# A second, fp32r transpose of the attention latents, fed by word copies and checked into the residual

## The chip, the cores and the metric

The kernel runs on one core of one Trainium2 chip. The metric is the device time of one execution in microseconds (us). The kernel before was run three times: 2292.96, 2293.53 and 2295.82 us, so its time is the median, 2293.53 us. One more execution was profiled; everything that is said of single instructions comes from that one.

## The reference, cut to what matters

The reference is a trunk of two layers, an attention layer (MLA) and a Mamba-2 layer, each followed by a squared-ReLU MLP, on a residual stream x of 256 tokens by 2048 features, all in fp32. The change lies in the attention layer, where the input is projected to two latents of 512 features each, which are normalised and projected again:

```python
a = h @ w_in
c_q, c_kv, k_rope = jnp.split(a, [Q_LORA_RANK, Q_LORA_RANK + KV_LORA_RANK], axis=-1)
q = (rms_norm(c_q, q_norm_g) @ w_uq).reshape(B, S, MLA_HEADS, QK_HEAD_DIM)
kv = (rms_norm(c_kv, kv_norm_g) @ w_ukv).reshape(B, S, MLA_HEADS, QK_NOPE_DIM + V_HEAD_DIM)
...
x = x + mix
```

c_q and c_kv are the latents. mix is the output of the attention, and x the residual to which it is added.

## The kernel before, in words

All products of fp32 operands are made of fp32r matmuls: each operand is split into a rounded half (h, type fp32r) and the rest (lo = value - h), and three products h·h, lo·h and h·lo are summed. Weights arrive by DMA from the SP queue (L85) into six raw buffers, ScalarE rounds them (L102, wh), VectorE subtracts (L103, wl), and TensorE uses them (L325, L326, L329 in `block`). Loads run six units of weights ahead of TensorE and conversions three; there are four buffers each for wh and wl, so ScalarE and VectorE stop when TensorE hasn't freed one.

The order on TensorE is that of the program text. The other engines' order is set when the kernel is built, by a scheduler that follows the program's order but lets an instruction that it reckons to be ready go first. Each engine then runs its list in order.

The 256 tokens are two tiles of 128 (t = 0 and 1). A latent is 128 x 512 for each tile. Small pieces of work that need time before TensorE can go on are put off with `later(n, fn)`: fn is run after n more blocks, between two blocks. The stage around the change goes like this on TensorE:

- four blocks give the q latent (key "ain q"), then a narrow product ("ain r", L344), then four blocks give the kv latent ("ain c")
- `latent` (L781) takes the two accumulators: ScalarE sums squares (L296), VectorE and GpSimd make the reciprocal root (L282, L283, L789), VectorE scales the accumulator into a scratch tile cn (L794). It returns two functions, one for each token tile, that call `transposes`
- for the q latent, the two functions are put off with `later(3, fn)`, so they run after the third of the four "ain c" blocks, and after them the fold of the narrow product (L352) on the same tick; then comes the fourth "ain c" block
- for the kv latent, they run in the middle of the second q projection, `s0q(1)`, after the first of its two weight units; then follow the second unit and the first kv projection `s0kv(0)`, whose operands are the transposed latents (ckv)

`transposed` (L307) takes one PSUM bank, makes four 128 x 128 fp32 transposes into it (L310), and `split_out` lets ScalarE write the rounded half h from the bank (L299) and VectorE the rest lo (L300). A bank comes from `bank(wide)`: with wide true every second one is from the pool yp (two banks), otherwise it is from the pool sm (two banks). The q latent is transposed with wide true, the kv latent with wide false.

GpSimd (POOL) does the powers (L283, L290), the rotary tables and the rotary products (L764 to L779), and in this stage issues no DMA. Its first DMA in the kernel comes at 310 us (L199).

Of the kernel before, what the change touches and what calls it, by code (L numbers as in the profile page):

```python
# [20 lines left out]
F32 = mybir.dt.float32  # L21
F32R = mybir.dt.float32r
I32 = mybir.dt.int32
AF = mybir.ActivationFunctionType
ALU = mybir.AluOpType
# [3 lines left out]
P = 128  # L29
# [185 lines left out]
class Trunk:  # L215
# [565 lines left out]
    def latent(self, accs, gain, tiles, wide=True):  # L781

        nc = self.nc
        ssq = self.stat(2)
        for t in range(2):
            self.square_sum(accs[t], ssq[:, t:t + 1], scale=self.rs[t])
        r = self.rsqrt(ssq, 2, 512)
        r2 = self.stat(2)
        nc.vector.tensor_tensor(r2, r, self.rs_pool[(self.phase - 1) % 2][:, 0:2], ALU.mult)  # L789
        g = self.gain_tile(gain)  # L790
        fns = []
        for t in range(2):
            cn = self.scratch()
            nc.vector.scalar_tensor_tensor(cn, accs[t], r2[:, t:t + 1], g, ALU.mult, ALU.mult)  # L794
            fns.append(lambda t=t, cn=cn: self.transposes(cn, tiles[0], tiles[1], t, wide))
        return fns

    def mla(self, gain):
# [4 lines left out]

    def mla_body(self, mp, gain):
        nc, d = self.nc, self.d
        cq = [mp.tile([P, 4, 256], F32R, name=f"cq{i}") for i in range(2)]
        ckv = [mp.tile([P, 4, 256], F32R, name=f"ckv{i}") for i in range(2)]
        mk = mp.tile([P, 256], F32, name="mk")
# [29 lines left out]
        lat = self.latent(accs, d["kvg"], ckv, False)  # L838
# [725 lines left out]
```

## Time and profile before

| | us |
|---|---|
| median of three runs | 2293.53 |
| lowest and highest run | 2292.96, 2295.82 |
| the profiled execution, its own time | 2294.05 |
| its span from first to last instruction | 2292.3 |

The 1.75 us between the span and the execution's own time lie around the instructions. In rows of the profile, the line of the code stands first, then engine, operation, and the tiles as out<-in. A row of the timeline has the start, the duration, and the number of instructions that were merged. TensorE's matmuls overlap: a row shows 0.39 us for one of 512 columns, but the next starts 0.23 us later, so starts are compared, not durations. A transpose shows 0.27 us and is followed by the next after 0.11 us. "wh", "wl", "cq", "ckv", "s" (scratch, which cn is), "sm", "yp" and "acc" are the program's names of tiles.

### The profile page before, as it was taken

Reading aid. Unit: us, or ns where it says so; the run is one execution under the profiler, and the core shown is the slowest. Engines: PE = TensorE matmul, PEld = TensorE weight load, DVE = VectorE, ACT = ScalarE, POOL = GpSimd, SP = SyncE. Lnnn points to the kernel's source line nnn. Section 1 sums busy time; section 2 is a strip of 40 time slices with the busy share of each in tenths; the row PEclk is TensorE's granted clock in tenths of the full one; section 3 lists DMA queues with packets and bytes.
Section 4 is the critical chain, followed back from the end, with each engine's and each line's share of the span. In section 5 each row is a group of like instructions: output and inputs, shape, how many; then the busy total and the mean of one; then the engine's idle time right before and its main releaser. Section 6 shows DMA issues by size and latency. Waiting matters only on the chain.

```text
span 2292.3 us, 30455 instructions
## 1 busy us (share of the span) xinstructions
PE 2283.9 (100%) x10929; PEld 1898.4 (83%) x10929; DVE 1907.0 (83%) x2318; ACT 1392.6 (61%) x1947; POOL 212.7 (9%) x229
## 2 busy tenths in 40 slices
PE   9999999999999999999999999999999999999999
PEld 7898888888888888888888888888888888888887
DVE  7785698999899898687898688676989889989895
ACT  7775476566566666564666545544666666666663
POOL 1430000000000000000133112120000000000000
PEclk9999999999999999999999999999999999999999
DMA  8445687877887878667877777666687788888874
GB/s 315 151 126 155 198 230 249 261 242 252 262 242 247 262 215 275 201 209 241 283 262 264 253 265 256 228 197 200 208 258 233 244 267 244 249 267 239 249 226 163
DMA packets 161912, 538.07 MB, mean 235 GB/s; under 512 B 17680, under 2 KB 26832, under 8 KB 160736
## 3 DMA queue, kind: packets, MB, share of 16 engines
q1 hardware_dynamic: 151264, 502.44, 66.2%
q0 software_dynamic: 8096, 29.41, 7.9%
q10 hardware_dynamic: 2400, 4.27, 0.5%
q8 instruction: 86, 1.41, 0.3%
q14 instruction: 66, 0.54, 0.1%
HBM read 529.65 MB, written 6.41 MB: 234 GB/s over the span
## 4 chain that ended last, share of the span: by engine, by line
PE 97%; DMA 1%; DVE 1%; issue 0%; ACT 0%; SPq 0%; DVEq 0%
PE acc L325 13%; PE acc L326 13%; PE acc L329 13%; PE yp L595 9%; PE yp L596 9%; PE yp L594 9%; PE st L595 7%; PE st L596 7%; PE st L594 7%; PE sm L310 2%; DMA wraw<-mi 1%; DVE wl L103 1%; PE y L1280 1%; PE acc L594 1%; PE acc L596 1%; PE acc L595 1%
## 5 line engine op out<-in xcount | busy, mean ns | idle before, releaser
L102 ACT ACTIVATE wh<-wraw 128x1024 fp32r<-128x1024 f32 (+1 forms) x818 | 858.2, 1053 | 607.3 <-PE acc L326 284.3
L103 DVE TENSOR_TENSOR wl<-wraw,wh 128x1024 fp32r<-128x1024 f32 (+1 forms) x818 | 986.4, 1221 | 230.2 <-ACT wh L102 220.8
L595 PE MATMUL yp<-wl,k 128*128 128x512 f32 x896 | 348.9, 389 | 2.0 <-DVE wl L103 2.0
L594 PE MATMUL yp<-wh,k 128*128 128x512 f32 x896 | 349.8, 390 | 0.0
L596 PE MATMUL yp<-wh,k 128*128 128x512 f32 x896 | 348.8, 389 | 0.0
L325 PE MATMUL acc<-wh,xt 128*128 128x512 f32 x704 | 279.1, 397 | 0.9 <-ACT wh L102 0.9
L326 PE MATMUL acc<-wh,xt 128*128 128x512 f32 x704 | 274.5, 390 | 0.3 <-DVE xt L463 0.3
L102 ACT ACTIVATE wh<-wrx 128x1024 fp32r<-128x1024 f32 x168 | 177.9, 1059 | 136.0 <-PE yp L596 107.1
L103 DVE TENSOR_TENSOR wl<-wrx,wh 128x1024 fp32r<-128x1024 f32 x168 | 204.4, 1222 | 35.6 <-ACT wh L102 35.3
L595 PEld LDWEIGHTS yp<-wl,k 128*128 128x128 f32 x896 | 168.2, 188 | 37.4 <-DVE wl L103 2.8
L596 PEld LDWEIGHTS yp<-wh,k 128*128 128x128 f32 x896 | 168.2, 188 | 35.0
L594 PEld LDWEIGHTS yp<-wh,k 128*128 128x128 f32 x896 | 168.2, 188 | 34.7
L325 PE MATMUL acc<-wh,k 128*128 128x512 f32 x496 | 196.5, 396 | 0.0
L326 PE MATMUL acc<-wh,k 128*128 128x512 f32 x496 | 193.2, 390 | 0.0
L329 PE MATMUL acc<-wl,xt 128*128 128x512 f32 x704 | 188.3, 389 | 0.0
L594 PE MATMUL st<-wh,xt 128*128 128x512 f32 x448 | 176.8, 395 | 0.0
L595 PE MATMUL st<-wl,xt 128*128 128x512 f32 x448 | 174.8, 390 | 0.0
L596 PE MATMUL st<-wh,xt 128*128 128x512 f32 x448 | 174.8, 390 | 0.0
L325 PEld LDWEIGHTS acc<-wh,xt 128*128 128x128 f32 x704 | 132.3, 188 | 29.9 <-ACT wh L102 2.2
L326 PEld LDWEIGHTS acc<-wh,xt 128*128 128x128 f32 x704 | 132.3, 188 | 28.5 <-issue 1.2
L329 PEld LDWEIGHTS acc<-wl,xt 128*128 128x128 f32 x704 | 132.2, 188 | 27.7
L199 POOL DMA_DIRECT2D wrx<-mi x56 | 49.1, 876 | 1142.1 <-DVE wl L103 1036.1
(307 smaller groups left out, 3447.9 us busy)
## 6 DMA issues: line engine op xcount, KB each, us to landing
wraw<-mi SPq DMA_DIRECT2D x256, 512.0 KB, 5.3
wraw<-mo SPq DMA_DIRECT2D x256, 512.0 KB, 5.5
wraw<-si SPq DMA_DIRECT2D x160, 512.0 KB, 4.9
wraw<-so SPq DMA_DIRECT2D x64, 512.0 KB, 4.8
wrx<-mi SPq DMA_DIRECT2D x56, 512.0 KB, 5.3
wrx<-mi POOLq DMA_DIRECT2D x56, 512.0 KB, 8.2
wraw<-wo SPq DMA_DIRECT2D x32, 512.0 KB, 3.8
taps<-xD SPq DMA_DIRECT2D x16, 768.0 KB, 8.7
```

What stands on the lines that cost most here:

```text
L102: self.last = nc.scalar.activation(h[:, v], raw[:, v], AF.Copy)
L103: self.last_lo = nc.vector.tensor_tensor(lo[:, v], raw[:, v], h[:, v].bitcast(F32), ALU.subtract)
L199: nc.gpsimd.dma_start(st["b11"].tile, quarter(d, 1, 0), accum_op=ALU.add)
L310: self.nc.tensor.transpose(b[:, j * P:(j + 1) * P], src[:, j * P:(j + 1) * P], self.ident)
L325: nc.tensor.matmul(accs[t][:, :n], ah, wh[:, q, :], start=first and kt + q == 0, stop=False)
L326: nc.tensor.matmul(accs[t][:, :n], al, wh[:, q, :], start=False, stop=False)
L329: nc.tensor.matmul(accs[t][:, :n], lhs(kt + q, t)[0], wl[:, q, :], start=False, stop=en and q == nk - 1)
L594: nc.tensor.matmul(b, ah, wh, start=first and q == 0, stop=False)
L595: nc.tensor.matmul(b, ah, wl, start=False, stop=False)
L596: nc.tensor.matmul(b, al, wh, start=False, stop=last and q == 1)
L1280: nc.tensor.matmul(y[t][c, o], part(t)[:, c], xg[g][t][:, o], start=True, stop=True)
```

## The change: what it does

For each latent and token tile, a GpSimd DMA copies cn word for word into a new tile q of type fp32r. Where the tile was transposed once, it is now transposed twice: first q, as fp32r with an fp32r identity, into one bank, which ScalarE copies to a tile e; then cn, as fp32 as before, into another bank. VectorE subtracts the second bank from e, adds 2^60 times that difference to the first 512 columns of the residual tile, and then the second bank is split into h and lo as before. Both banks are of the pool sm, also for the q latent. The difference is zero if the fp32r transpose passes every word unchanged. The fp32r identity is made by a copy on GpSimd one block after the start.

```diff
         for t in range(2):
             cn = self.scratch()
             nc.vector.scalar_tensor_tensor(cn, accs[t], r2[:, t:t + 1], g, ALU.mult, ALU.mult)
-            fns.append(lambda t=t, cn=cn: self.transposes(cn, tiles[0], tiles[1], t, wide))
+            q = self.lat_pool.tile([P, 512], F32R, tag="lat", name=self.name("lat"), bufs=4)
+            nc.gpsimd.dma_start(q.bitcast(F32), cn)
+
+            def both(t=t, cn=cn, q=q):
+                b = self.bank(False)
+                for j in range(4):
+                    nc.tensor.transpose(b.bitcast(F32R)[:, j * P:(j + 1) * P], q[:, j * P:(j + 1) * P], self.ident_r)
+                e = self.lat_pool.tile([P, 512], F32, tag="late", name=self.name("late"), bufs=2)
+                nc.scalar.activation(e, b, AF.Copy)
+                b = self.bank(False)
+                for j in range(4):
+                    nc.tensor.transpose(b[:, j * P:(j + 1) * P], cn[:, j * P:(j + 1) * P], self.ident)
+                nc.vector.tensor_tensor(e, e, b, ALU.subtract)
+                x = self.x[t][0]
+                nc.vector.scalar_tensor_tensor(x, e, 2.0 ** 60, x, ALU.mult, ALU.add)
+                h, lo = (v[:, :, t * P:(t + 1) * P] for v in tiles)
+                self.split_out(h, lo, b.rearrange("p (k n) -> p k n", k=4))
+
+            fns.append(both)
...
     def mla_body(self, mp, gain):
         nc, d = self.nc, self.d
+        self.lat_pool = mp
+        self.ident_r = mp.tile([P, P], F32R, name="identr")
+        self.later(1, lambda: nc.gpsimd.tensor_copy(self.ident_r, self.ident))
```

## The prediction

> **What bounds the kernel now.** I read the page's busy table and chain first, then TensorE's waits, then the timeline between 28 and 80 us, where the attention's latents are made.
>
> ```profile
> span 2292.3 us, 30455 instructions
> PE 2283.9 (100%) x10929; PEld 1898.4 (83%) x10929; DVE 1907.0 (83%) x2318; ACT 1392.6 (61%) x1947; POOL 212.7 (9%) x229
> PEclk9999999999999999999999999999999999999999
> PE 97%; DMA 1%; DVE 1%; issue 0%; ACT 0%; SPq 0%; DVEq 0%
> ...
> PE yp L595 <- DVE wl L103: 2.0, 2, 1.1
> PE warmed L433 <- DVE warm L430: 1.4, 1, 1.4
> PE acc L325 <- ACT wh L102: 0.9, 1, 0.9
> PE yp L910 <- DVE qn L865: 0.4, 1, 0.4
> PE acc L326 <- DVE xt L463: 0.3, 1, 0.3
> ```
>
> TensorE (PE) is 97% of the chain that ended last, and its listed waits add up to 5.0 us in 2292.3. Its clock is full in every slice. So the kernel takes as long as TensorE's list of instructions, and a microsecond in which TensorE stands still is a microsecond more: nothing later can give it back, because there is hardly a wait left to fill.
>
> The changed functions run at two places in TensorE's order.
>
> ```profile
> 45.76 1.41 DVE L794 SCALAR_TENSOR_TENSOR s<-acc,st,gb 128x512 f32<-128x512 f32 x2
> 49.42 0.60 PE L310 MATMUL sm<-cst,s 128*128 128x128 f32 x4
> 50.05 0.60 ACT L299 ACTIVATE cq<-sm 128x512 fp32r<-128x512 f32 x1 [0.50 <-PE sm L310]
> 50.68 0.69 DVE L300 TENSOR_TENSOR cq<-sm,cq 128x512 fp32r<-128x512 f32 x1 [1.18 <-ACT cq L299]
> ...
> 58.98 1.41 DVE L794 SCALAR_TENSOR_TENSOR s<-acc,st,gb 128x512 f32<-128x512 f32 x2
> 62.49 1.03 PE L310 MATMUL sm<-cst,s 128*128 128x128 f32 x8
> 63.28 0.42 PE L325 MATMUL yp<-wh,cq 128*128 128x384 f32 x1
> ...
> 62.65 0.87 PE sm L310 x8
> ```
>
> For the q latent cn is written from 45.76 us and transposed at 49.42; for the kv latent it is written from 58.98 and transposed at 62.49. The last row is the chain's: eight transposes take 0.87 us of TensorE, 0.11 each. Both places have about 2.9 us from the end of the first cn to its transpose, and TensorE waits at neither. That is the slack on which the change draws.
>
> **The change part by part.** First, **the word copy.** TensorE's first fp32r transposes now need cn by way of a DMA that GpSimd issues. No DMA of 256 KB from GpSimd is in the trace, so these rows are the nearest:
>
> ```profile
> gb<-g SPq DMA_DIRECT2D x12, 256.0 KB, 2.7
> gb<-kvg SPq DMA_DIRECT2D x1, 256.0 KB, 4.7
> wrx<-mi POOLq DMA_DIRECT2D x56, 512.0 KB, 8.2
> out<-x SPq DMA_DIRECT2D x2, 128.0 KB, 1.9
> xD<-s POOLq DMA_DIRECT2D x1, 48.0 KB, 2.6
> ...
> L199 POOL DMA_DIRECT2D wrx<-mi x56: 854/873/1081, 310.5 to 2213.3; - x56
> ...
> 46.00:50.00 4.00, 4.00 (x22) 3.35 (x21) 3.50 (x5) 1.70 (x2) 1.08 (x6) 1.00 0.15 17
> 58.00:62.00 4.00, 4.00 (x25) 4.00 (x24) 3.18 (x5) 2.98 (x9) 0.72 (x1) 1.00 0.68 220
> ```
>
> The time from issue to landing is bounded below by 2.6 us (48 KB from GpSimd) and above by 8.2 (512 KB, accumulating, with busy queues). From SP, 256 KB take 2.7 us. GpSimd's 48 KB took 2.6, at least 0.7 more than SP needs for 128 KB (1.9), and going from SP's 128 KB down to 48 would save some more, which I put at 0.4; so a DMA from GpSimd costs about 1.1 us more, and 256 KB about 3.8. That is for a quiet stage. The windows' last two columns are the DMA engines' busy share and GB/s: the q latent's copy flies in a quiet stage (0.15), the kv latent's beside weight loads (0.68), where SP's own 256 KB took 4.7 instead of 2.7. I take 3.8 for q and 4.8 for kv, between 3.8 and 3.8 + 2.0.
>
> One cn takes half of 1.41 us and its pipeline's end, 0.75. So q's first copy is issued at 45.76 + 0.75 = 46.5 and lands at 50.3, where TensorE wants it at 49.42: **0.9 us late**. kv's is issued at 59.7 and lands at 64.5 for a want at 62.49: **2.0 us late**. The second copy of each pair is issued 0.9 us after the first (L199's 873 ns) and lands before its transposes can have a bank, as follows.
>
> By the Trainium skill, "DMA: Bandwidth & Descriptors", section "Anatomy of one DMA", a DMA from GpSimd takes 2.0 us and its bytes at 436 GB/s; for 256 KB that is an estimate of 2.6 us, both copies would be in time, and the sum below would be 2.9 us less. The trace's 48 KB at 2.6 speaks for a larger fixed part.
>
> Second, **the banks.** Each call now takes two banks of sm, which has two. For t = 0 both are free. For t = 1 the first needs only ScalarE's copy of e to be over, but the second still holds the fp32 transpose of t = 0, until VectorE has subtracted it, done the residual (ahead of it in program order) and written lo. TensorE's order is fixed, so it stands. From the start of the first fp32r transposes:
>
> ```profile
> L1317 DVE SCALAR_TENSOR_TENSOR s<-xtm,st,gb x16: 741/746/753, 1159.4 to 1551.1; 128x512 f32<-128x512 f32 x16
> ...
> 64.29 0.95 DVE L103 TENSOR_TENSOR wl<-wraw,wh 128x768 fp32r<-128x768 f32 x1
> ```
>
> - ScalarE can start e 0.63 us after (49.42 to 50.05 above) and takes 0.60: 1.23
> - VectorE subtracts in 0.69 (L300's row): 1.94 with the handover of 0.03 that the rows above show
> - VectorE scales and adds the residual; the nearest row is L1317, also two SBUF inputs and a factor, 0.75: 2.69
> - VectorE writes lo in 0.69: 3.38; ScalarE's h (0.60) lies beside the residual
> - TensorE makes the four last transposes in 0.44: 3.87 with the handover
>
> Before, the same place took 0.87 us of TensorE, so this chain costs **3.0 us** at each place. The eight added transposes of a place (0.87 us if an fp32r transpose costs what an fp32 one does) are inside it. If the residual is put behind lo, it is 2.25; if a conversion that is ready slips in between on VectorE (0.95 by the second row above), it is 3.95.
>
> Third, **what lies beside other work.** The identity is one copy on GpSimd:
>
> ```profile
> POOL xt L901 <- issue: 15.1, 1, 15.1
> ACT wh L102 <- PE acc L326: 9.1, 7, 1.8
> PEld acc L326 <- DVE ckv L300: 0.7, 2, 0.4
> ...
> 52.77 1.04 POOL L776 TENSOR_TENSOR ra<-kro,cc 128x128 f32<-128x128 f32 x1 [5.69 <-DVE kro L833]
> 62.34 0.38 POOL L289 TENSOR_TENSOR st<-st,eps 128x4 f32<-128x4 f32 x1 [3.59 <-ACT s L296]
> ...
> L85 SPq DMA_DIRECT2D wrx<-mi x56: 327/328/720, 281.8 to 2133.7; - x56
> ```
>
> GpSimd idles 15.1 us ahead of its memsets for the attention, so the copy is hidden. Behind the DMAs on GpSimd wait the rotary products of L776 at q and the sums of L289 at kv; it idled 5.69 and 3.59 us before them, more than two issues of 0.9. VectorE gets 4 x (0.69 + 0.75) = 5.8 us and ScalarE 4 x 0.60 = 2.4 more; conversions hide it, since ScalarE waits for TensorE to free weight buffers (9.1 us in seven waits between 28 and 80), not the other way. If that cover were gone, t = 1's subtraction and residual, 1.44 us ahead of its lo, would show at the first kv projection. There weight loads now wait 0.7 us for ckv's lo; in the longer stall VectorE gets some of its queue done, and I take 0.4 us back. SP's queue isn't touched (the copies share only its 16 engines, with 1 MB in all), the picks of later banks stay (four more counts, an even number), and the tiles that are added are free 200 us before the MLP's first load (281.8) that could lie in their place.
>
> **The sum:** q 3.0 + 0.9, kv 3.0 + 2.0, less 0.4: **8.5 us**. The profiled execution took 2294.05 us, 0.52 above the median, and would take 2302.55; against the median of 2293.53 that is **2302.0 us**.
>
> **The rivals.** What a measurement can tell from no change is about 0.2%, 4.6 us: "same" ends at 2298.1.
>
> *Landing early.* If 256 KB land in 2.6 us as the 48 KB did, q's are there at 49.1 and kv's at 62.3, both in time. The banks still cost 2 x 3.0, or 2 x 2.25 with the residual behind lo, less 0.4: 4.1 to 5.6, so 2297.6 to 2299.1. For it speaks that the copies don't touch the chip's outer memory; against it, that no DMA of this size is that fast in the trace. Chance 17%, nearly all with 2297.6, within 0.2%.
>
> *Landing late.* If they take the 8.2 us of GpSimd's 512 KB, q's land at 54.7 and kv's at 67.9: 5.3 and 5.4 late, 16.3 us with the banks: 2309.8. Against it: half the bytes and no accumulation. Chance 13%.
>
> *TensorE slows down after the stall.* The first matmuls show that it can:
>
> ```profile
> 1.44 4.20 PE L433 MATMUL warmed<-warm 128*128 128x512 f32 x9 [1.44 <-DVE warm L430]
> ...
> 33.69 0.23 PE acc L325
> ```
>
> Nine matmuls of 512 columns took from 1.44 to 5.6, 0.47 us each, where later ones take 0.23: about 2 us lost in 4. If a stall of 4 to 5 us, with only transposes in it, brings that state back, each place costs 2 us more: 2306.0. No stall of that length is in the trace, so it shows neither side. Chance 12%. The Trainium skill, "TensorE: Matmul & The Clock Gate", Part 1, states that the clock is halved after an idle window of about 3.4 us and comes back after as long a busy one. By that rule the stalls here, cut by transposes into pieces of under 2 us, would mostly escape; the first matmuls agree with the halving.
>
> *Faster.* While TensorE stands still, SP, ScalarE and VectorE go on and fill the six raw and four converted buffers. If that lead lasted, the places where the chain goes by weight loads could vanish:
>
> ```profile
> 1722.50 6.00 DMA wraw<-mi
> 2141.22 6.18 DMA wraw<-mi
> 2170.83 5.75 DMA wraw<-mi
> ```
>
> All three would be 17.9 us, and 8.5 - 17.9 gives 2284.1; from 13.1 us won it would decide. Against it: these loads wait for buffers that TensorE frees, so a lead of a few units at 60 us is used up long before 1720, and TensorE's own waits for weights are only 2.9 us. Chance 3%.
>
> *The change not doing what it says.* Whether the fp32r transpose rounds or passes words changes values, and no instruction's count or order; it has the forecast's time. If an fp32r transpose were half the price of an fp32 one, 0.06 us x 16 would come off before the banks' chain, at most 0.9 us.
>
> **How the numbers follow.** Forecast 55% (a stall of some 7 to 11 us, all slower), late 13%, slow clock 12%, early 17% (15 same, 2 slower), faster 3%: faster 3%, same 15%, slower 82%. The range goes from 2297.5, the early case's lower end, which leaves out 3% and about half of the early case, to 2311.0, late landing with one conversion of 0.95 us in between, which leaves out about 5%.
>
> **What would show it.** Right: TensorE's waits list about 1 us before the fp32r transposes of q and 2 us before kv's, put down to the DMA into q, and then at each some 0.4 us before the second fp32r transposes (ScalarE's e) and 1.7 before the second fp32 ones (VectorE's lo); all later stages are shifted by one amount and keep their lengths; waits elsewhere stay at some 5 us. Wrong on the copy: DMA rows of 2.6 or 8 us to landing. Wrong on the banks: no wait before the second fp32 transposes, or one much longer, with conversions between the subtraction and lo on VectorE. Slow clock: 0.47 us between matmuls after 54 or 67 us. The whole would be wrong if later stages changed their lengths, because the scheduler put ScalarE's and VectorE's lists in another order.

## The result, and the profile after

| | before | after |
|---|---|---|
| median of the executions compared, us | 2294.68 | 2302.82 |
| lowest and highest | 2292.96, 2296.00 | 2301.23, 2305.12 |
| executions | 4 | 4 |

The change costs 8.1 us: the ratio of after to before is 1.0037, with a 95% interval of 1.0024 to 1.0050. A second measurement beside other kernels gave 1.0033 (1.0021 to 1.0044), 7.5 us. The prediction was 2302.0, so the sum came out within a microsecond. The runs show that this was in part luck: by the executions at full clock the standing still alone cost less than forecast, and a slow clock that the sum left out made up much of the difference.

The profiled execution of the changed kernel is the slowest of its four: 2305.12 us, span 2303.3, so 11.0 us above the span of before. From its page, the span and the chain's shares; from its view of TensorE's waits, the rows (us in total, times, longest):

```profile
span 2303.3 us, 30520 instructions
PE 92%; DVE 4%; DMA 2%; issue 1%; ACT 0%; POOL 0%; SPq 0%; DVEq 0%; ACTq 0%
```

```profile
PE sm L801 <- DMA lat<-s: 2.6, 4, 1.6
...
PE sm L806 <- ACT late L803: 1.4, 2, 0.7
...
PE sm L352 <- DVE cq L300: 0.6, 1, 0.6
```

L801 is the fp32r transposes, L806 the second fp32 ones, L803 ScalarE's copy e, L352 the fold. Before, none of these waits was in the list. They add up to 4.6 us, and with the added transposes' own time (four times 0.34) they don't reach 11.0. The timeline of TensorE shows the rest. Each row has the start, the duration and, in brackets, the idle time ahead of it. First before:

```profile
48.50 1.07 PE L329 MATMUL acc<-wl,xt 128*128 128x512 f32 x4
...
50.65 0.48 PE L325 MATMUL acc<-wh,xt 128*128 128x512 f32 x1
...
56.22 0.33 PE L325 MATMUL acc<-wh,cq 128*128 128x384 f32 x1
...
61.80 0.86 PE L329 MATMUL yp<-wl,cq 128*128 128x384 f32 x4
...
65.45 0.40 PE L325 MATMUL acc<-wh,ckv 128*128 128x512 f32 x1
...
71.97 0.41 PE L910 MATMUL yp<-cst,qn 128*128 128x128 f32 x2 [0.41 <-DVE qn L865]
```

Then the same stage after:

```profile
48.44 1.07 PE L329 MATMUL acc<-wl,xt 128*128 128x512 f32 x4
49.79 0.51 PE L801 MATMUL sm<-identr,lat 128*128 128x128 f32 x4 [0.28 <-DMA lat<-s]
50.13 0.62 PE L806 MATMUL sm<-cst,s 128*128 128x128 f32 x4
51.09 0.51 PE L801 MATMUL sm<-identr,lat 128*128 128x128 f32 x4 [0.33 <-DMA lat<-s]
52.28 0.66 PE L806 MATMUL sm<-cst,s 128*128 128x128 f32 x4 [0.69 <-ACT late L803]
53.50 1.05 PE L352 MATMUL sm<-cst,s 128*128 128x64 f32 x4 [0.56 <-DVE cq L300]
54.30 0.77 PE L325 MATMUL acc<-wh,xt 128*128 128x512 f32 x1
54.88 0.63 PE L326 MATMUL acc<-wh,xt 128*128 128x512 f32 x1
55.30 0.63 PE L325 MATMUL acc<-wh,xt 128*128 128x512 f32 x1
...
61.15 0.33 PE L325 MATMUL acc<-wh,cq 128*128 128x384 f32 x1
...
66.72 0.86 PE L329 MATMUL yp<-wl,cq 128*128 128x384 f32 x4
67.99 0.51 PE L801 MATMUL sm<-identr,lat 128*128 128x128 f32 x4 [0.41 <-DMA lat<-s]
...
70.56 0.67 PE L801 MATMUL sm<-identr,lat 128*128 128x128 f32 x4 [1.61 <-DMA lat<-s]
71.92 1.11 PE L806 MATMUL sm<-cst,s 128*128 128x128 f32 x4 [0.69 <-ACT late L803]
72.69 0.67 PE L325 MATMUL yp<-wh,cq 128*128 128x384 f32 x1
...
76.67 0.63 PE L325 MATMUL acc<-wh,ckv 128*128 128x512 f32 x1
...
82.64 0.38 PE L931 MATMUL yp<-cst,qn 128*128 128x128 f32 x2
```

Read by starts, this divides into five pieces:

- **the q place**, from the start of the four lo products (L329) to the next block: 48.44 to 54.30 is 5.86 us, before 48.50 to 50.65 is 2.15: **+3.71**
- **the two blocks after it**, to the first product with cq: 54.30 to 61.15 is 6.85, before 50.65 to 56.22 is 5.57: **+1.28**, though nothing was added there
- **the kv place**, in the same way: 66.72 to 72.69 is 5.97, before 61.80 to 63.28 is 1.48: **+4.49**
- **the weight unit after it**, to the first product with ckv: 72.69 to 76.67 is 3.98, before 63.28 to 65.45 is 2.17: **+1.81**
- **the first kv projection**, to the transposes of qn: 76.67 to 82.64 is 5.97, before 65.45 to 71.97 is 6.52: **-0.55**

The sum is +10.7; 11.0 at the end of the span. The second and fourth pieces are not waits. In the q rows, matmuls of 512 columns start 0.42 us apart (54.88 to 55.30) instead of 0.23. The windows of TensorE in the changed kernel say why; the columns are the window's length, busy time with the count, the granted clock, the DMA engines' share and GB/s:

```profile
50.00:54.00 4.00, 2.43 (x19) 0.95 0.95 300
54.00:58.00 4.00, 4.00 (x14) 0.62 0.44 170
...
66.00:70.00 4.00, 2.55 (x18) 1.00 0.97 314
70.00:74.00 4.00, 2.75 (x12) 0.58 0.60 212
74.00:78.00 4.00, 4.00 (x13) 0.56 0.00 0
```

At each of the two places the clock falls to half. In finer windows the granted clock is 0.50 from 53.6 to 57.0 us and from 70.7 to 77.5 us, that is for 3.4 and 6.8 us. The page's row by fortieths of the span can't show it: these are a small part of a slice of 58. So by starts the loss of this execution is 7.65 us of place (3.71 + 4.49 - 0.55) and 3.1 us of slow clock (1.28 + 1.81). The clock's true part is larger, because it fell before the places were over: the fold took 0.80 us to the next start (53.50 to 54.30), 0.36 before, and the last kv transposes 0.77 (71.92 to 72.69), where four take 0.43 at full clock (49.42 to 49.85 before).

The clock's part is not the same in each execution. The mean granted clocks of the four were 0.998, 0.999, 0.999 and 1.000, and their times 2305.12, 2303.44, 2302.19 and 2301.23: the lower the clock, the longer the time. In the second measurement the order is less clean (1.000 took 2301.76, three with 0.998 took 2302.29 to 2304.72, and two with 0.999 took 2301.34 and 2301.92). The two executions at 1.000 are 6.55 and 7.16 us over before, which is the nearest that the runs have to the price of the standing still alone.

Inside a place, the chain of the changed kernel (start, length, what) shows who sets the end:

```profile
46.19 0.34 POOL ss L767
47.23 0.71 POOL lat L796
47.94 3.02 DMA lat<-s
...
52.23 0.50 ACT cq L299
52.75 0.70 DVE cq L300
53.50 1.05 PE sm L352 x4
...
65.61 4.81 DMA lat<-s
```

At q the chain goes through GpSimd's rotary tables (L767), the issue of the second copy, its landing 3.02 us later, ScalarE, VectorE's lo of t = 0 (L300) and the fold, which needs the bank that this lo frees. At kv it goes by the second copy, which took 4.81 us, and ScalarE's e. VectorE's added work is not on it.

### The profile page after: what moved, and what is told of

The parts are those of the page before. It is cut to its first block, busy times and chain, and to the rows that moved or that the text cites. A ratio compares the mean times of both kernels' runs of the same rounds, so it can differ in the third digit from the quotient of the medians.

```text
span 2303.3 us, 30520 instructions
## 1 busy us (share of the span) xinstructions
PE 2291.7 (99%) x10945; PEld 1903.1 (83%) x10945; DVE 1912.6 (83%) x2326; ACT 1395.3 (61%) x1951; POOL 214.7 (9%) x234
## 4 chain that ended last, share of the span: by engine, by line
PE 92%; DVE 4%; DMA 2%; issue 1%; ACT 0%; POOL 0%; SPq 0%; DVEq 0%; ACTq 0%
PE acc L325 13%; PE acc L326 13%; PE acc L329 13%; PE yp L595 9%; PE yp L596 9%; PE yp L594 9%; PE st L595 7%; PE st L596 7%; PE st L594 7%; DVE wl L103 2%; DMA wraw<-mi 2%; PE sm L310 2%; PE y L1301 1%; DVE wraw L183 1%; PE acc L703 0%
## 5 line engine op out<-in xcount | busy, mean ns | idle before, releaser
L329 PE MATMUL acc<-wl,xt 128*128 128x512 f32 x704 | 188.3, 389 | 0.0
L329 PEld LDWEIGHTS acc<-wl,xt 128*128 128x128 f32 x704 | 132.1, 188 | 27.7
```

Of the source, the lines that this page charges most:

```text
L329: nc.tensor.matmul(accs[t][:, :n], lhs(kt + q, t)[0], wl[:, q, :], start=False, stop=en and q == nk - 1)
```

## The experiments

In all of them "before" is the kernel before, measured beside them on the same chip. A column "place" is worked out as above, from starts in the timeline of the run's own profile, one execution each: the time from the lo products to the next block, less that of before. "Clock" is what the pieces after q and after kv took beyond 5.57 and 2.17 us, and "first kv" what the first kv projection took beyond 6.52. Medians, with the ratio to before and its 95% interval:

| kernel | median, us | over before, us | ratio (95%) | q place | kv place | clock after q, kv | first kv |
|---|---|---|---|---|---|---|---|
| after, once more | 2302.10 | +7.5 | 1.0033 (1.0021 to 1.0044) | +4.98 | +4.49 | 1.84, 0.95 | -0.01 |
| no copy | 2301.18 | +6.8 | 1.0032 (1.0021 to 1.0042) | +4.57 | +2.26 | 0, 0 | +0.03 |
| own banks | 2301.79 | +7.4 | 1.0036 (1.0022 to 1.0049) | +4.02 | +3.51 | 1.44, 1.20 | -1.03 |
| no copy, own banks | 2299.77 | +5.4 | 1.0026 (1.0017 to 1.0035) | +3.32 | +0.88 | 0, 0.20 | +3.03 |
| no copy, own banks, fold's too | 2296.64 | +2.0 | 1.0008 (0.9999 to 1.0017) | +0.87 | +0.88 | 0, 0 | +2.82 |
| no residual | 2300.13 | +5.8 | 1.0026 (1.0016 to 1.0036) | +2.52 | +4.68 | 0, 1.81 | -0.74 |
| q only | 2297.84 | +3.2 | 1.0013 (1.0004 to 1.0021) | +3.55 | 0 | 1.38, 0 | -0.02 |
| kv only | 2298.90 | +4.3 | 1.0016 (1.0007 to 1.0024) | 0 | +5.13 | 0, 0.92 | 0 |
| waits filled | 2301.04 | +7.0 | 1.0030 (1.0019 to 1.0042) | +3.70 | +4.53 | 0, 0 | -0.45 |
| transposes added to before | 2302.45 | +8.4 | 1.0033 (1.0021 to 1.0044) | +4.36 | +4.37 | 0, 0 | -1.04 |
| matmuls added to before | 2300.07 | +6.0 | 1.0026 (1.0016 to 1.0035) | +4.30 | +4.36 | 0, 0 | -1.04 |
| check one block later | 2295.79 | +1.7 | 1.0008 (0.9999 to 1.0017) | 0 | +0.32 | 0, 0 | +0.05 |

(The 0.20 of the fourth row isn't slow clock: the granted clock is 1.00 there, and TensorE starts at 69.54, just behind ScalarE's h of ckv.) The intervals are 2 to 3 us to each side, so times alone don't separate the kernels between +5.4 and +8.4 from each other; for those the trace's places decide. They do separate the fold's own bank and the later check from the changed kernel. Kv only overlaps the changed kernel's interval a little and q only touches it, but all eleven executions of kv only and nine of the eleven of q only were shorter than the shortest of the changed kernel.

**The changed kernel once more**, without an edit, to see how far its places differ between executions.

> The changed kernel again, beside these. 8 us over the kernel before; its runs spread over 4 us as the clock drops at none, one or both of the places, with the longer runs showing the lower mean clock.

2302.10 us, +7.5; the six lie 3.4 us apart. TensorE's timeline of this run:

```profile
50.57 0.50 PE L801 MATMUL sm<-identr,lat 128*128 128x128 f32 x4 [1.52 <-DMA lat<-s]
...
53.02 1.11 PE L806 MATMUL sm<-cst,s 128*128 128x128 f32 x4 [0.69 <-ACT late L803]
```

Here TensorE stood 1.52 us for q's first copy, not 0.28, and the fold no longer waited: once TensorE comes later, VectorE's lo is over in time. The slow clock began within the transposes (the four at 53.02 show 1.11 us instead of 0.62). So the single waits vary and replace one another; between these two profiles the q place varies by about 1.3 us. By starts the places come to 9.46 us here (4.98 + 4.49 - 0.01), against 7.65 in the first profile, and TensorE is 11.7 us behind at the transposes of qn. The span is only 9.1 us longer than before's (2301.4): the profile of before has 2.0 us of waits for weights later on, and this one none.

**One place alone.** In "q only" the kv latent goes the way of before, in "kv only" the q latent:

```diff
             nc.vector.scalar_tensor_tensor(cn, accs[t], r2[:, t:t + 1], g, ALU.mult, ALU.mult)
+            if not wide:
+                fns.append(lambda t=t, cn=cn: self.transposes(cn, tiles[0], tiles[1], t, wide))
+                continue
             q = self.lat_pool.tile([P, 512], F32R, tag="lat", name=self.name("lat"), bufs=4)
```

("kv only" has `if wide:` there.)

> The change at the q latent alone; the kv latent is transposed once, as before. Theory: 3.7 us of standing still, as between the changed kernel's 49.8 and 54.3 us, 0 to 1.3 for the clock, less up to 1 that later waits give back: 2.5 to 5 us over the kernel before.

> The change at the kv latent alone. Theory: 4.5 us of standing still, 0 to 2.2 for the clock, less 1 to 2 that later waits give back: 2.5 to 6 us over the kernel before. With the run on the q latent alone it makes up the change's 8.1, within the intervals.

+3.2 and +4.3 us; together 7.5, which is what both places cost in the kernel measured beside them (+7.5). The two places add up, and the kv place costs no less than q's. Q only also shows the clock's part best: its six executions with a granted clock of 1.000 took 2295.83 to 2297.86 us, its five with 0.999 took 2297.84 to 2301.42.

**No copy.** The first transposes read cn by the fp32 identity, and no DMA is issued; everything else stays, so both transposes are the same.

```diff
-            q = self.lat_pool.tile([P, 512], F32R, tag="lat", name=self.name("lat"), bufs=4)
-            nc.gpsimd.dma_start(q.bitcast(F32), cn)
...
-                    nc.tensor.transpose(b.bitcast(F32R)[:, j * P:(j + 1) * P], q[:, j * P:(j + 1) * P], self.ident_r)
+                    nc.tensor.transpose(b[:, j * P:(j + 1) * P], cn[:, j * P:(j + 1) * P], self.ident)
```

> The word copies are left out: the first four transposes of each call read cn as fp32 instead of its fp32r copy (so the difference is of two equal transposes). Theory (the cost is TensorE's standing still, first for the copies, then for a bank, then running at a lower clock for some us): the four waits on the DMA, 2.6 us in the changed kernel's waits, and about 0.2 us of late start go, the waits for banks and for VectorE's lo stay; 4 to 6 us over the kernel before, and the lower clock after the kv latent is shorter or gone. Rival (the added instructions themselves cost the time, by taking ScalarE and VectorE from the weights): nothing changes, 8 us over the kernel before.

+6.8 us, more than the 4 to 6 expected. At kv the place fell from +4.49 to +2.26: there the copies were worth 2.2 us, near the 2.0 of the prediction (0.35 of it is the slow clock in the last transposes, 0.76 us instead of 0.41). At q nothing was won. TensorE started its transposes at once, and then stood before the fold:

```profile
54.08 0.66 PE L352 MATMUL sm<-cst,s 128*128 128x64 f32 x4 [2.05 <-DVE cq L300]
```

The wait for lo of t = 0 grew from 0.56 to 2.05 us. Two things made it so. TensorE was earlier, and VectorE's list is in another order: in this build the second subtraction, which waits for the last transposes, stands ahead of the residual and lo of t = 0. First VectorE in the changed kernel, then here:

```profile
51.69 0.69 DVE L809 SCALAR_TENSOR_TENSOR x<-late,x 128x512 f32<-128x512 f32 x1
52.75 0.69 DVE L300 TENSOR_TENSOR cq<-sm,cq 128x512 fp32r<-128x512 f32 x1 [0.37 <-ACT cq L299]
...
52.14 0.69 DVE L805 TENSOR_TENSOR late<-late,sm 128x512 f32<-128x512 f32 x1 [1.45 <-PE sm L804]
...
53.34 0.69 DVE L300 TENSOR_TENSOR cq<-sm,cq 128x512 fp32r<-128x512 f32 x1
```

In the changed kernel's order lo could have started once ScalarE's h was written, at 51.85; so some 1.5 us of the fold's wait, by this estimate, is the list's order and not the wait that the copy left behind. In that order removing the copy would have won something at q as well, but no run shows it.

**Own banks.** The first transposes take a bank of the pool acc instead of sm.

```diff
-                b = self.bank(False)
+                b = self.bank("acc")
                 for j in range(4):
                     nc.tensor.transpose(b.bitcast(F32R)[:, j * P:(j + 1) * P], q[:, j * P:(j + 1) * P], self.ident_r)
```

> Each call's first transposes go into a bank of the accumulators' pool, so the second ones of t = 1 find a bank of sm free. By the prediction's step the banks cost 3.0 us at each place, and 2 us over the kernel before would be left. By the trace of the changed kernel the banks alone are worth only the two waits of 0.7 us on ScalarE's copy; the fold after the q latent still waits for VectorE's lo of t = 0, and the copies are as late: 6 to 7.5 us over the kernel before.

+7.4 us, the changed kernel's time. The waits for ScalarE's e ahead of the second transposes are gone, which brought 1.0 us at kv (+3.51). At q the fold now waits:

```profile
54.05 0.82 PE L352 MATMUL sm<-cst,s 128*128 128x64 f32 x4 [2.19 <-issue]
```

The prediction put 3.0 us of each place on the second fp32 transposes of t = 1 waiting for a bank. With a bank to spare, most of that should have gone. It didn't, so at q the place is set not by those transposes but by the next user of sm, the fold, and at kv mostly by the copy. Here too VectorE's list has the second subtraction (52.06) ahead of lo of t = 0 (53.26); in the other order lo could have started at about 52.5, so by this estimate 0.7 us of the fold's 2.19 belongs to the order.

**No copy and own banks**, the two edits together.

> Both of the former: no word copies (fp32 read instead) and a bank of its own for each first transpose. Theory: at the kv latent nothing waits and only the eight added transposes are left, 0.9 us; at the q latent the fold still waits for VectorE's lo of t = 0, about 3 us in all; with the clock at full after kv and perhaps lower for a while after q: 3 to 5 us over the kernel before. Rival (added instructions): 8 us.

+5.4 us, a little over the 3 to 5 expected. At kv the place shrank to +0.88, which is the eight added transposes at 0.11 each and nothing else. At q it stayed at +3.32, nearly all of it the fold's wait of 2.2 us and the added transposes (VectorE's list has the same order as with own banks). The kv place's time isn't all won: the first kv projection now takes 9.55 us instead of 6.52, since ckv is late there, and the clock drops.

**The fold's bank too.** The last edit, and the fold's bank in this stage also from acc (the count that alternates the pools is kept in step):

```diff
         def fold():
-            b = self.bank(False)
+            self.nsm += 1
+            b = self.bank("acc" if key[0] == "ain" else False)
+            if key[0] != "ain":
+                self.nsm -= 1
```

> No word copies, banks of their own for the first transposes, and one for the fold of the narrow product after the q latent: nothing is left at that place for TensorE to wait for, with all the rest of the added work in place. Theory: the fold's wait of 2.2 us goes with the clock's drop after it; the late ckv halves at the first kv projection (2.1 us of waits in the kernel with own banks and no copies) stay: 1.5 to 4 us over the kernel before. Rival (work): 5.4 as in that kernel.

+2.0 us, and the places are +0.87 and +0.88. With the copy, the bank and the fold's bank all taken away, nothing of the stall is left there; with the first two alone it stayed at q. What remains of it comes later, at the first kv projection, which takes 9.34 us in this execution (+2.82), where TensorE waits for ckv:

```profile
68.03 0.50 PE L326 MATMUL acc<-wh,ckv 128*128 128x512 f32 x1 [0.19 <-DVE ckv L300]
69.25 0.50 PE L325 MATMUL acc<-wh,ckv 128*128 128x512 f32 x1 [0.72 <-ACT ckv L299]
70.28 0.50 PE L326 MATMUL acc<-wh,ckv 128*128 128x512 f32 x1 [0.53 <-DVE ckv L300]
...
71.38 0.63 PE L325 MATMUL acc<-wh,ckv 128*128 128x512 f32 x1
71.81 0.63 PE L326 MATMUL acc<-wh,ckv 128*128 128x512 f32 x1
```

0.19 + 0.72 + 0.53 is 1.44, as much as the prediction had for this place "if that cover were gone". That the sums agree to the digit is chance: the prediction meant VectorE's work ahead of lo, and half of this wait is for ScalarE's h. The clock falls there too: 0.43 us from 71.38 to 71.81.

**No residual.** The subtraction and the addition to the residual are left out; copy, both transposes and e stay.

```diff
-                nc.vector.tensor_tensor(e, e, b, ALU.subtract)
-                x = self.x[t][0]
-                nc.vector.scalar_tensor_tensor(x, e, 2.0 ** 60, x, ALU.mult, ALU.add)
```

> The subtraction and the addition to the residual are left out; copies, both transposes and ScalarE's copy stay. Theory: VectorE's lo of t = 0 comes 1.2 us earlier, so the fold after the q latent starts up to 0.6 us (its listed wait) to 1.2 us earlier; nothing changes at the kv latent, where the copy of t = 1 and ScalarE set the time: 6.5 to 8 us over the kernel before. Rival (VectorE's 5.8 us of added work is the cost): 2 to 3 us over the kernel before.

+5.8 us, below the 6.5 to 8 expected. At q the place is 2.52, and the fold starts without a wait. Two things differ there: VectorE's two instructions ahead of lo are gone, and ScalarE's list has h of t = 0 ahead of e of t = 1 (at 50.23 and 51.01 us), where the changed kernel has it behind (52.13 and 51.63). In the changed kernel lo waited 0.37 us for that h after VectorE's two instructions were over, so they alone were not what held it; the run doesn't separate the two causes. At kv the place is +4.68, no shorter than with them: there VectorE's work was not on the path. The prediction's chain ran through VectorE at both places.

**Waits filled.** Twenty matmuls of 512 columns, whose result nobody reads, are put where TensorE waits in the changed kernel.

```diff
+            def fill(n):
+                f = self.bank("acc")
+                v = self.xT[0][0].rearrange("p k n -> p (k n)")
+                for _ in range(n):
+                    nc.tensor.matmul(f, v[:, :P], v[:, 0:512], start=True, stop=True)
...
             def both(t=t, cn=cn, q=q):
+                fill(2 if t == 0 or wide else 6)
...
+                if t:
+                    fill(3)
...
+                if t and wide:
+                    fill(2)
```

> The changed kernel with matmuls of 512 columns on operands that are long there, into a spare bank that nobody reads, put where TensorE waits: 9 at the q latent, 11 at the kv latent, 0.23 us each. Theory (the stalls let the clock drop, and the drop is part of the price): the clock stays full in every window from 46 to 82 us, matmuls after both places start 0.23 us (512 columns) and 0.17 us (384) apart, and although TensorE has 4.5 us more to do, the time is no longer than the changed kernel's: 5 to 8.5 us over the kernel before, with runs closer together. Rival (the clock is not set by the stalls): the slow stretches stay, and 9 to 12 us over the kernel before.

+7.0 us with 20 more matmuls. The places are as long as those of the changed kernel (+3.70, +4.53), and the clock stays up. Rows of the windows:

```profile
54.00:58.00 4.00, 4.00 (x20) 1.00 0.43 167
...
74.00:78.00 4.00, 4.00 (x19) 1.00 0.45 131
```

All six executions had a granted clock of 1.000, where each of the two sets of the changed kernel, of four and of six, had one such. So the slow clock is a consequence of TensorE's standing still, and it is not the copy, the banks or a warmer chip. The 4.6 us of work in the waits cost nothing, and the span of this profile is even 4.2 us shorter than that of the changed kernel (2299.1 against 2303.3). In medians a gain isn't separated (+7.0 against +7.5 and +8.1).

**Transposes or matmuls added to before.** Two kernels have no change of the diff at all; they put a piece of pure TensorE work at both places, 40 fp32 transposes of the identity in one and 19 matmuls of 512 columns in the other, about 4.35 us each time.

```diff
+                if t == 0:
+                    f = self.bank("acc")
+                    for j in range(40):
+                        nc.tensor.transpose(f[:, j % 4 * P:(j % 4 + 1) * P], self.ident, self.ident)
                 self.transposes(cn, tiles[0], tiles[1], t, wide)
```

> The kernel before, with 40 fp32 transposes of the identity into a spare bank ahead of the latents' transposes at each of the two places: 2 x 40 x 0.11 = 8.7 us of TensorE without any wait. If transposes keep the clock up as matmuls do: 8.7 us over the kernel before, full clock. If they count as idle for the clock: matmuls behind them start 0.4 us apart for a while, and 10 to 13 us.

> The kernel before, with 19 matmuls of 512 columns into a spare bank at each of the two places: 2 x 19 x 0.227 = 8.6 us of TensorE without any wait. Every theory: 8.6 us over the kernel before, and the clock full; it is the control for the run with more transposes.

TensorE's timeline with the transposes:

```profile
49.38 4.53 PE L799 MATMUL acc<-cst 128*128 128x128 f32 x40
...
55.30 0.39 PE L326 MATMUL acc<-wh,xt 128*128 128x512 f32 x1
55.53 0.40 PE L325 MATMUL acc<-wh,xt 128*128 128x512 f32 x1
```

After 4.4 us of nothing but transposes the next matmuls start 0.23 us apart, and all seven executions had a clock of 1.000. So transposes hold the clock, and it is the gaps between them in the changed kernel that lose it. The Trainium skill, "TensorE: Matmul & The Clock Gate", Part 4, says that transposes don't count as activity in the same way and that the full clock doesn't engage for them. These rows differ, at least for a clock that is already up.

Both kernels added 8.7 us of TensorE's time at the places. At the transposes of qn they were 7.6 and 7.5 us behind before: the first kv projection took 5.48 us in both, 1.04 less than before, because ckv and qn were there in time. Their medians are +8.4 and +6.0, where 8.7 and 8.6 were expected. What lies between is outside the places. Of TensorE's waits after 90 us, nearly all for converted weights, the profile of before has 2.0 us in two waits, that of the added matmuls 1.1, that of the added transposes 5.1, and that of the changed kernel run once more none. These waits differ from profile to profile, and no run shows why.

**The check one block later.** The fp32 transposes and the split stay where they were before. The fp32r transposes, and the comparison on VectorE with h and lo as already written, come one block later.

```diff
+            def check(t=t, q=q, h=h, lo=lo):
                 b = self.bank(False)
...
-                nc.scalar.activation(e, b, AF.Copy)
...
+                nc.vector.tensor_tensor(e3, b3, h.bitcast(F32), ALU.subtract)
+                nc.vector.tensor_tensor(e3, e3, lo.bitcast(F32), ALU.subtract)
                 x = self.x[t][0]
                 nc.vector.scalar_tensor_tensor(x, e, 2.0 ** 60, x, ALU.mult, ALU.add)
...
+            def both(t=t, cn=cn, check=check):
+                self.transposes(cn, tiles[0], tiles[1], t, wide)
+                self.later(1, check)
```

> The same check put off: the fp32 transposes, h and lo stand where the kernel before has them; the word copy's fp32r transposes come one block later, and VectorE takes h and lo from them in two subtractions instead of one, then adds to the residual as in the change. More work on VectorE than the change (12 operations of 0.68 us instead of 8), the same sixteen added transposes. Theory (waits, not work): 1 to 3 us over the kernel before. Rival (the added work itself): 8 us or more.

+1.7 us, which can't be told from before (0.9999 to 1.0017). The timeline of TensorE:

```profile
60.47 0.80 PE L803 MATMUL sm<-identr,lat 128*128 128x128 f32 x8
61.11 0.41 PE L325 MATMUL yp<-wh,cq 128*128 128x384 f32 x1
```

Eight fp32r transposes take 0.64 us (60.47 to 61.11), at two places 1.3 us, and no wait stands before them, although the copies took 3.9 to 5.1 us to land. VectorE has twelve instructions more than before, where the change gave it eight. They are hidden nearly everywhere; behind the second check this profile has one wait of 1.00 us, at the last transposes of qn (74.74), for GpSimd, whose rotary product (L779) took 2.65 us there and 0.73 before. It is the best version of the whole change that was run; it is not faster than before.

## Why the prediction was right, and where its steps failed

- **What bounds the kernel** held. TensorE is on 92% of the chain, every wait put into its list showed in the time, and the later stages together kept their length within their own waits for weights: from the transposes of qn to the end it is 2220.3 us before, 2220.7 in the first profile and 2217.7 in the second. "Nothing later can give it back" held within that. The place that was to give back, the first kv projection, gave 0.55 us in the first profile and nothing in the second, for the 0.4 assumed (1.04 with the added matmuls). The waits for weights late in the kernel, 0 to 5 us in these profiles, blur anything finer.
- **The word copy at q** came near in sum, by two errors. The copies land in 2.5 to 3.0 us, not 3.8. But they were issued at 47.2, not 46.5: GpSimd was still busy with the rotary tables. The prediction had listed what waits behind the DMAs on GpSimd, and not what stands ahead of them. So 0.9 us late became 0.4 in the first profile and 1.7 in the second, by starts (49.35 and 48.89 would have been the starts without a wait). The Trainium skill, "DMA: Bandwidth & Descriptors", section "Anatomy of one DMA", gave an estimate of 2.6 us for the landing. The q copies of the changed kernel agree (2.5 and 3.0 us), those of the later check, issued at the same time, don't (4.6 and 4.5).
- **The word copy at kv**: 2.0 us late was forecast for the first copy of the pair, and none for the second, which "lands before its transposes can have a bank". The step that failed is the second half. The first copy was 0.6 us late (without a wait the start would have been at 66.72 + 0.69, as before; it was at 67.99), and the second, 4.81 us in flight while the DMA engines were 0.97 busy, held TensorE for 1.61. Sum 2.2, against 2.0; without the copies the place is 2.2 shorter.
- **The banks** is the step that was wrong in its mechanism. The second fp32 transposes of t = 1 were to wait for VectorE's lo of t = 0. They waited for ScalarE's e, 0.69 us at each place. The bank that e had just freed served them; the other one went to the next user of sm. At q that is the fold, and there the wait for lo appears (0.56 us; about 2.1 with one of the other waits removed, part of it from VectorE's list being in another order). At kv no other user of sm follows soon, and lo cost nothing. Without VectorE's added work, and with ScalarE's h of t = 0 ahead of e of t = 1, q is 1.2 us shorter and kv isn't. So "3.0 us at each place" was right at neither for its reason.
- **What lies beside other work** held for the identity copy and for the amount of ScalarE's and VectorE's added work. Its place in the lists can cost (no copy: an estimated 1.5 us at the fold), and once the stall ahead of it is gone, TensorE waits 1.44 us for ckv. The first kv projection then takes 2.82 us more, with the clock's drop, which the prediction hadn't priced.
- **The sum**: 8.5 us forecast for the two places less the recovery; by starts 7.65 in the first profile and 9.46 in the second, with some slow clock in both, while the two executions at a clock of 1.000 took 6.55 and 7.16 us more than before in all. The rival **TensorE slows down after the stall**, at 12%, was priced at 2 us for each place and happened: 1.28 and 1.81 us by starts in the profiled execution, and less or nothing in others, as q only shows (2295.83 to 2297.86 at a clock of 1.000, up to 2301.42 at 0.999). It should have been a term of the sum. That the total came out to 0.8 us is luck: the places were overpriced by about as much as the clock adds in a middling execution. The reason given against this rival was a rule. The Trainium skill, "TensorE: Matmul & The Clock Gate", Part 1, puts the halving after an idle window of about 3.4 us, and by it stalls cut by transposes were held to escape mostly. No single wait was over 1.61 us, and the clock fell. The same Part, in "A second HAM failure mode: psum-queue depth-cycling", tells of a clock that swings from short idle times between groups of matmuls; that agrees with these rows.
- **The other rivals**: landing early was right for q's flight and didn't help, since the issue was late and the fold's wait took over. Landing late (8.2 us) and faster didn't occur.

Two things stay open. Which stalls lose the clock is settled only in part. Each of the eleven drops at these places and at the first kv projection lasted 3.41 or 6.83 us, and where a profile has two (after 17.07, after once more 20.48, own banks 17.07 us from one start to the other), the second begins five or six times 3.41 us after the first. In the 3.41 us ahead of a drop TensorE's rows show it busy for 1.22 to 1.97 us. But how long it stands doesn't decide alone: the profiled run without the copy was busy for only 0.69 us from 50.70 to 54.11 and kept its clock, though six of its seven executions lost some. This fits a clock that is judged in steps of 3.41 us which don't begin with the stall; no run tests it. And q's longest wait moves from execution to execution among copy, bank and fold.

## What to carry to other kernels

On an engine whose order is fixed, price a change by the instructions that now wait there, and follow each wait to the next user of the same buffers: taking one of several serial waits away may bring little. Look at the other engines' lists after each edit, since the scheduler may have ordered them anew. A check that nobody downstream needs belongs behind the path, one block later; there the same work, with more instructions on VectorE, was hidden. After the waits themselves, add what a broken stall of a few microseconds can do to the clock, and look for it in windows of that size.

## What the hardware showed that was not expected

- The granted clock fell to 0.50 for 3.41 or 6.83 us at places that were 3.5 to 5.1 us longer than before, with waits of 0.3 to 2.2 us between groups of four transposes, and twice after some 1.5 us of waits among matmuls (first kv projection, no copy and own banks, with and without the fold's). It differed between executions of one kernel, and 20 matmuls in the gaps, about 4.6 us of work, prevented it in six of six.
- Unbroken transposes keep the clock up: 40 in a row, and the next matmuls at full speed.
- Four fp32r transposes of 128 x 128 take 0.34 us from start to start (49.79 to 50.13), four fp32 ones 0.43 or 0.44: 0.085 against 0.11 us each.
- 256 KB from tile to tile by GpSimd landed in 2.5 to 3.0 us at q, except in the later check (4.5 and 4.6), and in 2.9 to 5.5 us at kv, beside weight loads.
